# A two-layer decoder trunk on one core: rests shared otherwise, scaling in steps, gathered rows moved from one stage to the next

## The chip, the cores and the metric

The kernel runs on one core of a Trainium2 chip. Five engines work side by side, each with its own queue of instructions: TensorE (PE, with its weight loads as PEld), VectorE (DVE), ScalarE (ACT), GpSimd (POOL) and SyncE (SP). Transfers are issued from the queues of SP, ACT and POOL. The metric is the time of one execution on the device, in microseconds; less is better.

## The reference, cut to what matters

Two layers over 256 positions of width 1024. The even layer's mixer is attention and retention, the odd layer's a short gated convolution; after each mixer comes PEER, a retrieval of 16 out of 16384 experts for each of 8 heads.

```python
def short_conv_mixer(xn, w_in, conv_w, w_out):
    bg, cg, hx = jnp.split(xn @ w_in, 3, axis=-1)
    u = cg * hx
    y = lax.conv_general_dilated(u, conv_w[:, None, :], ...)
    return (bg * y) @ w_out

def peer(xn, w_q, sub_keys, u, v):
    q = (t @ w_q).reshape(n_tok, PEER_HEADS, 2, PEER_DKEY // 2)
    sc = jnp.einsum('thpd,hpnd->thpn', q, sub_keys).astype(jnp.float32)
    s1, i1 = lax.top_k(sc[:, :, 0], PEER_TOPK)
    s2, i2 = lax.top_k(sc[:, :, 1], PEER_TOPK)
    ...
    eidx = jnp.take_along_axis(cidx, pos, axis=-1)
    gate = jax.nn.softmax(top_s, axis=-1).astype(xn.dtype)
    ...
        hid = jax.nn.gelu(jnp.einsum('td,thkd->thk', tc, u[ec]), approximate=False)
        return jnp.einsum('thk,thkd->td', gc * hid, v[ec])
```

So each token needs, for its 128 chosen experts, a product with a row of u, a GELU, a gate, and a weighted sum of rows of v. All values are float32.

## The kernel before, in words

The 256 tokens are treated in two ways. For 160 of them (`TD`) PEER is computed densely: the whole of u and of v, 128 tiles each of 128 experts, goes through TensorE, and the gates of experts that were not chosen are zero. For the other 96 (`TG`) the rows of the chosen experts are gathered from memory by index. 96 gathered steps for u and 96 for v make 192 steps in a layer; each step brings 128 rows of 4 KB (0.5 MB, as much as one tile of u or v).

The order of the work is written out by hand; each engine runs its instructions in the order of the program. The stages of a layer are:

- **Mixer** (even or odd). Weights come as float32 tiles `raw`, at most eight at a time, and each is split into a part `hi` that TensorE takes at a higher rate (ScalarE, L144) and a rest `lo` in bf16 (L146). Whether VectorE or GpSimd subtracts the rest is the second entry of a tile's source: True means GpSimd. For the odd mixer's W_in that is the list on L210. The splits run two tiles ahead of TensorE's use, four in the mixers.
- **Joint.** At the end of a stage four quarters of the sum are added to h, each followed by `norm.done(a, ...)`; the new h is transposed (`turn`) and split with its gain (`parts`) into x2, the operand of the next stage. `amid` runs between two parts of the last quarter, and `tail` finishes inside the first pair of projections of the next stage (`u_pair`).
- **Queries.** Sixteen projections with W_q, scores against the sub-keys, and top-k on VectorE. `rows` (L473) makes the dense tokens' operand XF and the gathered tokens' XG, at the second projection.
- **u stage.** For each tile i of u: eight matmuls (L1223), GELU on ScalarE, and from about the 60th tile on the gate matrices G (L1186), which need one-hot masks from VectorE (L1178). Meanwhile `Gather.step` consumes gathered rows: VectorE multiplies a row (L866 for u, L881 for v), and POOL issues the row that takes its buffer (L856), six buffers in all. How many steps are consumed at each tile is set by `ga.rate`, so that about `UPTO` are done before the last eleven tiles.
- **v stage.** For each tile of v, 40 of 128 are multiplied whole (L1312), at four passes; 88 (`SPL`) are split into vhi (ScalarE, L1234) and vlo (VectorE, L1241), and the hidden rows likewise into hs and hb (ScalarE, L1288 and L1289) and a rest of hs (VectorE, L1293, `row_rest`), and multiplied in two kinds of matmul (L1316 with hs, L1318 with hb). Parts are made three tiles ahead (`AHEAD`). The gathered steps that remain are consumed here at an even rate; then everything is folded into h.

Of the kernel before, what the change touches and what calls it, by code (L numbers as in the profile page):

```python
# [9 lines left out]
F32 = mybir.dt.float32  # L10
# [4 lines left out]
OP = mybir.AluOpType  # L15
# [3 lines left out]
P = 128  # L19
S = 256  # L20
D = 1024
ND = D // P
# [5 lines left out]
NK = 128  # L28
# [6 lines left out]
TG = 96  # L35
TD = S - TG
STEPS = TG
SUB = 32
# [2 lines left out]
MORE = 4  # L41
GT = 4
SCR = 11 * D
UPTO = 132
SPL = [i for i in range(NK) if i % 2 or i % 16 in (4, 8, 12)]
CODE = 64.0
WHOLE = 1.5 * 2.0 ** 23
PRE = {5 * k: k for k in range(11)} | {58: 14, 64: 15, 70: 11, 76: 16, 82: 18, 88: 12, 94: 17, 100: 13, 106: 19}
# [2 lines left out]
CALM = 11  # L51
# [51 lines left out]
class Stream:  # L103
# [28 lines left out]
    def whole(self, i):  # L132
        return self.srcs[i][1] is None
# [49 lines left out]
def trunk_kernel(ctx, tc, x, small, cst, mcst, ew_in, ew_out, ow_in, ow_out, wq, keys, pu, pv, pun, gains, out):  # L183
    nc = tc.nc
    v = nc.vector
    act = nc.scalar
    gp = nc.gpsimd
# [8 lines left out]
    srcs = []  # L196
# [10 lines left out]

    srcs += peer_srcs(0)
    OF = [b * ND + k for k in range(ND) for b in (1, 2, 0)]
    srcs += [(ow_in[f], i not in (1, 2) and i % 4 != 3) for i, f in enumerate(OF)]  # L210
    srcs += [(ow_out[c], c % 2 == 0 and c < 6) for c in range(ND)]
    srcs += peer_srcs(1)

    h = pers.tile([P, 2, D], F32, tag="h", name="h")
# [6 lines left out]
    XF = pers.tile([P, ND, TD], F32, tag="xf", name="xf")  # L221
    XG = pers.tile([P, 2, D], F32, tag="xg", name="xg")
# [5 lines left out]
    def hid_tile(name):  # L228
        return ps_hid.tile([P, 512], F32, tag="hid", name=name)
# [9 lines left out]
    def nm(s):  # L239
        uid[0] += 1  # L240
        return f"{s}{uid[0]}"
# [17 lines left out]
    def u_pair(A2, Ab, tail):  # L259


        ws = [st.next(ahead=False) for _ in range(2)]
        pss = [hid_tile(nm("hid")) for _ in range(2)]
        for k in range(ND):
            for s_ in range(2):
                for (hi, lo), ps in zip(ws, pss):
                    pe.matmul(ps[:, :S], hi[:, k * P:(k + 1) * P], A2[:, k, s_, :], start=k == 0 and s_ == 0,
                              stop=False)
            if k == 0:
                tail()  # L270
                st.ahead(0)
        for (hi, lo), ps in zip(ws, pss):
            for k in range(ND):
                pe.matmul(ps[:, :S], lo[:, k * P:(k + 1) * P], Ab[:, k, :], start=False, stop=k == ND - 1)
        return pss
# [58 lines left out]
    def new_x2():  # L334
        xv["x2"] = pers.tile([P, ND, 2, S], F32R, tag="x2", name=nm("x2"))

    class Sums:


        def __init__(self):  # L340
            self.w = pers.tile([P, 2, 8], F32, tag="nw", name=nm("nw"))
# [29 lines left out]
    class Norm(Sums):  # L371
# [3 lines left out]
        def __init__(self, gi):  # L375
            super().__init__()
            self.gi = gi
            self.ps = {}
            self.turned = False

        def warm(self):

# [29 lines left out]
        def done(self, a, junk):  # L412

            if a == 1:
                self.turn(0)
            if a < 3:
                self.square(a, junk)
            if a == 1:
                self.mean0(0)
                self.root(0)  # L420
            if a == 2:
                self.turn(1)
                self.rstd(0)
                self.mean0(1)
                new_x2()
            if a == 3:
                if not self.turned:
                    self.turn(2)
                self.parts(0)
                self.junk = junk  # L430

        def amid(self):

            self.turn(2)
            self.turned = True

        def tail(self):

            self.turn(3)
            self.parts(1)  # L440
            self.square(3, self.junk)
            self.root(1)
            self.rstd(1)
# [28 lines left out]

        def rows(self):  # L473

            ps = self.spread()
            x2 = xv["x2"]
            v.tensor_tensor(XF, x2[:, :, 0, TG:].bitcast(F32), x2[:, :, 1, TG:].bitcast(F32), OP.add)
            v.tensor_tensor(XF, XF, ps[:, None, TG:].to_broadcast([P, ND, TD]), OP.mult)
            v.scalar_tensor_tensor(XG[:TG, 0, :], h[:TG, 0, :], self.scale(0)[:TG], XG[:TG, 1, :],
                                   op0=OP.mult, op1=OP.mult)  # L480
            act.copy(XG[:TG, 1, :], XG[:TG, 0, :])
            for q in range(2):
                gp.dma_start(XG[TG:, q, :], XG[q * SUB:(q + 1) * SUB, 0, :])

    class Final(Sums):

# [10 lines left out]
        def gained(self, a, eng):  # L497
            th, c = a // 2, slice(a % 2 * 512, (a % 2 + 1) * 512)
            eng.tensor_tensor(self.xs[:, th, c], h[:, th, c], self.g[:, c], OP.mult)

        def done(self, a, junk):
            self.square(a, junk)
# [400 lines left out]
    def peer(l, before, norm):  # L903
        with tc.tile_pool(name=nm("hg"), bufs=1) as hp:
            HG = hp.tile([P, NK, TD], F32, tag="hg", name=nm("hg"))
# [35 lines left out]
            ga = Gather(hp)  # L941
# [56 lines left out]
            def stage1(th, f0, f1):  # L998
                def g():
                    top16([(V[th][:, f * TK:(f + 1) * TK], IU[th][:, f * TK:(f + 1) * TK],  # L1000
                            sc(th, f)) for f in range(f0, f1)])
                return g
# [129 lines left out]
            for f in range(NPAIR):  # L1132
                if f == 0:
                    pair = u_pair(xv["x2"], Xb, before.tail)
                ps = pair[f] if f < 2 else u_tile(xv["x2"], Xb)
                act.copy(qT[f % 2], ps[:, :S])
                if f == 1:
                    before.rows()
                if f:
                    scores(f - 1)  # L1140
                    pump.add((1.35, stage1(0, f - 1, f)))
                    if f <= HH * 2:
                        pump.add((1.35, stage1(1, f - 1, f)))
                    if f == HH * 2:
                        chain(0, 0)
                        pump.add((0.6, lambda: places(0)))
                    if early:
                        fetch(early.pop(0))
                pump.run(3.2)
# [48 lines left out]
            gst = {"g": -1, "credit": 0.0, "rate": 0.0}  # L1198
# [45 lines left out]
            for i in range(NK):  # L1244
                ps = dense_u(i)
                if i == 0:
                    after_first()
                elif early_u:
                    fetch(early_u.pop(0))
                if i == NK - 1:  # L1250
                    gst["rate"] = 1.0
                    while gst["g"] < NG:
                        slot(i)
                T = max(gst["g"], 0) * GT
                if T < TD:
                    act.activation(HG[:, i, T:], ps[:, T:TD], AF.Gelu)  # L1256
                if T > 0:
                    act.activation(ps[:, :T], ps[:, :T], AF.Gelu)
                    v.tensor_tensor(HG[:, i, :T], ps[:, :T], HG[:, i, :T], OP.mult)  # L1259
                slot(i + 1)  # L1260
                if gst["g"] < 0:
                    if i == first_late - 2:
                        pump.flush()
                    if pump.q:
                        pump.run(1.4)
                    else:
                        gst["g"] = 0
                        gst["rate"] = NG / (2.0 * (NK - 8 - i))
                        onehots(0)
                        onehots(1)  # L1270
                ga.rate = 0.85 if gst["g"] < 0 else (UPTO - ga.c) / (NK - CALM - i) if i < NK - CALM else 0.6
                if i < NK - QUIET:
                    ga.step()
                elif i in (NK - QUIET, NK - QUIET + 2):
                    weight_parts(i - NK + QUIET + 1)
# [14 lines left out]

            def row_rest(j):
                hs = hsb[j][0]
                v.tensor_tensor(hs[:, 1, :], HG[:, j, :], hs[:, 0, :].bitcast(F32), OP.subtract)  # L1293

            for j in (1, 3):
                row_parts(j)
                row_rest(j)
            for i in range(NK):
                j = i + AHEAD
                if 4 <= j and j in SPL:  # L1300
                    weight_parts(j, False)
                    row_parts(j)
                if 4 <= j - 1 and j - 1 in SPL:
                    weight_rest(j - 1)
# [4 lines left out]
                m = dict(start=i == 0, skip_group_check=True)  # L1309
                if i not in SPL:  # L1310
                    for b in range(ND):
# [18 lines left out]
            for a in range(4):  # L1330
                th, ch = a // 2, a % 2
                for b in range(4):
                    pe.transpose(fq[a][:, b * P:(b + 1) * P], OT[:, ch * 4 + b, th * P:(th + 1) * P], ident)
                c = slice(ch * 512, (ch + 1) * 512)
                v.tensor_tensor(h[:, th, c], fq[a], h[:, th, c], OP.add)
                norm.done(a, fq[a])
            vpool.close()

    with tc.manual_schedule():
# [12 lines left out]
        a = Norm(1)  # L1352
# [3 lines left out]
        a = Norm(3)  # L1356
# [40 lines left out]
```

## Time and profile before

| | |
|---|---|
| median of 3 runs | 1529.94 us (1529.59 to 1531.46) |
| the profiled execution | 1531.33 us, its span 1529.6 us |
| TensorE busy | 1468.2 us, 96% of the span |
| VectorE, ScalarE, GpSimd busy | 1206.3, 790.9 and 676.0 us |
| moved by DMA | 533.03 MB, 348 GB/s on average |

TensorE's busy time counts pipelined records that overlap, so 96% does not mean that it runs at its peak; the pace of equal records tells more. In lines of the groups the columns are the source line, the engine, the operation, what it writes and reads, the count, the busy time, the mean duration of one in ns, and the idle time before it with what ended it.

### The profile page before, as it was taken

Reading aid. Unit: us, or ns where it says so; the run is one execution under the profiler, and the core shown is the slowest. Engines: PE = TensorE matmul, PEld = TensorE weight load, DVE = VectorE, ACT = ScalarE, POOL = GpSimd, SP = SyncE. Lnnn points to the kernel's source line nnn. Section 1 sums busy time; section 2 is a strip of 40 time slices with the busy share of each in tenths; the row PEclk is TensorE's granted clock in tenths of the full one; section 3 lists DMA queues with packets and bytes.
Section 4 is the critical chain, followed back from the end, with each engine's and each line's share of the span. In section 5 each row is a group of like instructions: output and inputs, shape, how many; then the busy total and the mean of one; then the engine's idle time right before and its main releaser. Section 6 shows DMA issues by size and latency. Waiting matters only on the chain.

```text
span 1529.6 us, 30523 instructions
## 1 busy us (share of the span) xinstructions
PE 1468.2 (96%) x11094; PEld 1375.5 (90%) x11108; DVE 1206.3 (79%) x2561; ACT 790.9 (52%) x2020; POOL 676.0 (44%) x521
## 2 busy tenths in 40 slices
PE   9999999989999999999979999999899999999997
PEld 5667999989999999999969789999899999999996
DVE  5647999868898787777785589996778887787886
ACT  5555512158777354545553463213787754555454
POOL 6744544446655232322046364454556652323310
PEclk9999999999999999999989999999999999999998
DMA  8544899999999999999955568999999999999993
GB/s 320 198 143 178 318 408 408 398 404 408 407 397 409 372 402 375 399 403 393 323 185 194 187 222 332 408 408 400 407 407 405 406 396 383 407 399 402 407 394 127
DMA packets 147576, 533.03 MB, mean 348 GB/s; under 512 B 16993, under 2 KB 17249, under 8 KB 147425
## 3 DMA queue, kind: packets, MB, share of 16 engines
q1 hardware_dynamic: 72144, 258.36, 44.1%
q0 software_dynamic: 56704, 205.07, 34.2%
q10 hardware_dynamic: 18576, 67.64, 11.4%
q8 instruction: 88, 1.44, 0.4%
q14 instruction: 64, 0.52, 0.1%
HBM read 528.34 MB, written 1.05 MB: 346 GB/s over the span
## 4 chain that ended last, share of the span: by engine, by line
PE 35%; DMA 32%; DVE 23%; issue 7%; ACT 2%; POOL 1%; ACTq 0%; DVEq 0%; POOLq 0%
DMA raw<-pv 14%; DMA rows<-pun,ig 7%; PE vo L1316 7%; DMA rows<-pv,ig 6%; PE vo L1312 5%; PE hid L1223 5%; DMA grow<-pun,ig 4%; DVE rows L866 3%; PE vo L1318 3%; PE hid L250 3%; DVE hg L982 2%; DVE grow L866 2%; PE ea L284 2%; DVE hg L988 2%; DVE hg L984 2%
## 5 line engine op out<-in xcount | busy, mean ns | idle before, releaser
L1223 PE MATMUL hid<-xf,raw 128*128 128x160 f32 x3456 | 492.3, 301 | 0.2
L1223 PEld LDWEIGHTS hid<-xf,raw 128*128 128x128 f32 x3456 | 478.7, 192 | 0.8 <-issue 0.5
L1234 ACT CAST vhi<-raw 128x1024 fp32r<-128x1024 f32 x176 | 184.2, 1046 | 231.6 <-DMA raw<-pv 176.3
L1241 DVE TENSOR_TENSOR vlo<-raw,vhi 128x1024 bf16<-128x1024 f32 x176 | 215.4, 1224 | 109.5 <-ACT vhi L1234 86.0
L856 POOL DMA_INDIRECT rows<-pv,ig x128 | 158.8, 1241 | 268.5 <-DVE gacc L881 233.7
L1316 PE MATMUL vo<-hs,vhi 128*128 128x320 f32 x1408 | 251.6, 320 | 6.1 <-DVE hs L1293 5.9
L146 POOL TENSOR_TENSOR lo<-raw,hi 128x1024 bf16<-128x1024 f32 x75 | 178.3, 2394 | 90.1 <-ACT hi L144 88.2
L1316 PEld LDWEIGHTS vo<-hs,vhi 128*128 128x128 f32 x1408 | 208.9, 188 | 9.2 <-DVE hs L1293 9.1
L856 POOL DMA_INDIRECT rows<-pun,ig x128 | 156.1, 1219 | 130.5 <-DVE rows L866 85.1
L1312 PE MATMUL vo<-hg,raw 128*128 128x160 f32 x1280 | 190.5, 302 | 0.9 <-DVE hg L1259 0.9
L866 DVE SCALAR_TENSOR_TENSOR rows<-rows,xg 128x1024 f32<-128x1024 f32 x128 | 155.6, 1220 | 39.1 <-DMA rows<-pun,ig 36.1
L1312 PEld LDWEIGHTS vo<-hg,raw 128*128 128x128 f32 x1280 | 176.3, 190 | 1.2 <-DVE hg L1259 1.2
L1256 ACT ACTIVATE hg<-hid 128x160 f32<-128x160 f32 (+25 forms) x242 | 63.1, 269 | 210.5 <-PE hid L1223 165.1
L881 DVE SCALAR_TENSOR_TENSOR gacc<-rows,ghid,gacc 128x1024 f32<-128x1024 f32 x124 | 158.7, 1279 | 10.2 <-DMA rows<-pv,ig 9.4
L1177 ACT ACTIVATE ko<-ko,idxT 128x128 f32<-128x128 f32 x320 | 130.8, 481 | 0.0
L856 POOL DMA_INDIRECT grow<-pv,ig x64 | 77.0, 1203 | 118.3 <-DVE gacc L881 99.4
L1318 PE MATMUL vo<-hb,vlo 128*128 128x160 bf16 x1408 | 128.3, 234 | 0.0
L1174 ACT ACTIVATE ko<-cst,idxT 128x128 f32<-128x128 f32 x320 | 103.1, 391 | 36.3 <-PE G L1186 31.9
L250 PE MATMUL hid<-x,hi 128*128 128x256 f32 x800 | 108.9, 289 | 6.7 <-issue 6.7
L144 ACT CAST hi<-raw 128x1024 fp32r<-128x1024 f32 x100 | 102.6, 1048 | 19.0 <-issue 10.1
L1186 PE MATMUL G<-ko 128*128 128x128 f32 x640 | 89.3, 284 | 24.0 <-DVE ko L1178 23.7
L1318 PEld LDWEIGHTS <-vlo 128*128 128x128 bf16 x1408 | 93.5, 98 | 18.0
(228 smaller groups left out, 2116.9 us busy)
## 6 DMA issues: line engine op xcount, KB each, us to landing
raw<-pu SPq DMA_DIRECT2D x216, 512.0 KB
raw<-pv SPq DMA_DIRECT2D x128, 512.0 KB
raw<-pv ACTq DMA_DIRECT2D x128, 512.0 KB
raw<-wq SPq DMA_DIRECT2D x32, 512.0 KB
raw<-ew_in SPq DMA_DIRECT2D x28, 512.0 KB
raw<-ow_in SPq DMA_DIRECT2D x24, 512.0 KB
hg<-pu SPq DMA_DIRECT2D x22, 512.0 KB
raw<-ew_out SPq DMA_DIRECT2D x8, 512.0 KB
```

The lines of the kernel that those rows point to most:

```text
L146: eng.tensor_tensor(lo, t, hi.bitcast(F32), OP.subtract)
L250: pe.matmul(ps[:, :S], hi[:, k * P:(k + 1) * P], A2[:, k, s_, :], start=k == 0 and s_ == 0, stop=False)
L856: gp.indirect_dma_start(self.row(s_), None, table, bass.IndirectOffsetOnAxis(IG[:, 0, s_ % STEPS:s_ % STEPS + 1].bitcast(U32), 0))
L866: v.scalar_tensor_tensor(r, r, 1.0, XG[:, q % 2, :], op0=OP.mult, op1=OP.mult, accum_out=w)
L881: v.scalar_tensor_tensor(self.acc[q], r, w, self.acc[q], op0=OP.mult, op1=OP.add)
L1177: act.activation(B[:, j], B[:, j], AF.Relu, bias=idxT[:, 2, t:t + 1], scale=idxT[:, 3, t:t + 1])
L1223: pe.matmul(ps[:, :TD], w[k], XF[:, k, :], start=k == 0, stop=k == ND - 1)
L1234: act.copy(whi[j], raw)
L1241: v.tensor_tensor(wlo[j], raw, whi[j].bitcast(F32), OP.subtract)
L1312: pe.matmul(vo[b][:, :TD], w[:, b * P:(b + 1) * P], HG[:, i, :], stop=False, **m)
L1316: pe.matmul(vo[b][:, :2 * TD], hi[:, b * P:(b + 1) * P], hs, stop=i == NK - 1, **m)
L1318: pe.matmul(vo[b][:, :TD], lo[:, b * P:(b + 1) * P], hb, stop=i == NK - 1, **m)
```

## The change: what it does

- `UPTO` becomes (126, 119), one number a layer, instead of 132 for both; with the few steps after it 130 and 123 steps are done in the u stages instead of 136, and 62 and 69 are left for the v stages instead of 56. Early in u the rate is 0.6 for eight tiles and then 0.88, instead of 0.85.
- `SPL` splits 95 tiles of v instead of 88.
- The rest of the hidden rows (`row_rest`) is subtracted by GpSimd, 190 times in all; VectorE had 176.
- In the odd mixer the rests of the first seven tiles of W_in all go to VectorE, and after that every second one to GpSimd: 9 of 24, where it had 16.
- `rows` gives back four steps, which run at the third to sixth projection, one at each.
- `tail` is called after two of eight steps of the first pair instead of one; `amid` makes the first two of the first four parts of x2, and is now also called at PEER's end, ahead of the last add.

```diff
-UPTO = 132
-SPL = [i for i in range(NK) if i % 2 or i % 16 in (4, 8, 12)]
+UPTO = (126, 119)
+SPL = [i for i in range(NK) if i % 2 or i % 4 == 0 and i > 0]
...
-    srcs += [(ow_in[f], i not in (1, 2) and i % 4 != 3) for i, f in enumerate(OF)]
+    srcs += [(ow_in[f], i > 6 and i % 2 == 1) for i, f in enumerate(OF)]
...
-            if k == 0:
+            if k == 1:
                 tail()
                 st.ahead(0)
...
             if a == 3:
-                if not self.turned:
-                    self.turn(2)
-                self.parts(0)
+                self.parts(0, (2, 3))
                 self.junk = junk
 
         def amid(self):
 
             self.turn(2)
-            self.turned = True
+            self.parts(0, (0, 1))
...
         def rows(self):
 
-            ps = self.spread()
             x2 = xv["x2"]
-            v.tensor_tensor(XF, x2[:, :, 0, TG:].bitcast(F32), x2[:, :, 1, TG:].bitcast(F32), OP.add)
-            v.tensor_tensor(XF, XF, ps[:, None, TG:].to_broadcast([P, ND, TD]), OP.mult)
-            v.scalar_tensor_tensor(XG[:TG, 0, :], h[:TG, 0, :], self.scale(0)[:TG], XG[:TG, 1, :],
-                                   op0=OP.mult, op1=OP.mult)
-            act.copy(XG[:TG, 1, :], XG[:TG, 0, :])
-            for q in range(2):
-                gp.dma_start(XG[TG:, q, :], XG[q * SUB:(q + 1) * SUB, 0, :])
+
+            def whole():
+                v.tensor_tensor(XF, x2[:, :, 0, TG:].bitcast(F32), x2[:, :, 1, TG:].bitcast(F32), OP.add)
+
+            def scaled():
+                ps = self.spread()
+                v.tensor_tensor(XF, XF, ps[:, None, TG:].to_broadcast([P, ND, TD]), OP.mult)
+
+            def fetched():
+                v.scalar_tensor_tensor(XG[:TG, 0, :], h[:TG, 0, :], self.scale(0)[:TG], XG[:TG, 1, :],
+                                       op0=OP.mult, op1=OP.mult)
+
+            def doubled():
+                act.copy(XG[:TG, 1, :], XG[:TG, 0, :])
+                for q in range(2):
+                    gp.dma_start(XG[TG:, q, :], XG[q * SUB:(q + 1) * SUB, 0, :])
+
+            return [fetched, doubled, whole, scaled]
...
                 if f == 1:
-                    before.rows()
+                    rows = before.rows()
+                if 1 < f < 6:
+                    rows[f - 2]()
...
-                ga.rate = 0.85 if gst["g"] < 0 else (UPTO - ga.c) / (NK - CALM - i) if i < NK - CALM else 0.6
+                ga.rate = (0.6 if i < 8 else 0.88) if gst["g"] < 0 else (UPTO[l] - ga.c) / (NK - CALM - i) if i < NK - CALM else 0.6
...
             def row_rest(j):
                 hs = hsb[j][0]
-                v.tensor_tensor(hs[:, 1, :], HG[:, j, :], hs[:, 0, :].bitcast(F32), OP.subtract)
+                gp.tensor_tensor(hs[:, 1, :], HG[:, j, :], hs[:, 0, :].bitcast(F32), OP.subtract)
...
                 c = slice(ch * 512, (ch + 1) * 512)
+                if a == 3:
+                    norm.amid()
                 v.tensor_tensor(h[:, th, c], fq[a], h[:, th, c], OP.add)
                 norm.done(a, fq[a])
```

More of the change, by code (lines that the diff above doesn't have):

```diff
@@ L378, in __init__ @@
             self.ps = {}
-            self.turned = False
         def warm(self):
@@ L499, in gained, with amid @@
             eng.tensor_tensor(self.xs[:, th, c], h[:, th, c], self.g[:, c], OP.mult)
+        def amid(self):
+            pass
         def done(self, a, junk):
```

## The prediction

> **What bounds the kernel now.** I read the page first (busy shares, data rate by slice), then the stretches of the stages, then the waits of TensorE, then the chain.
>
> ```profile
> span 1529.6 us, 30523 instructions
> PE 1468.2 (96%) x11094; PEld 1375.5 (90%) x11108; DVE 1206.3 (79%) x2561; ACT 790.9 (52%) x2020; POOL 676.0 (44%) x521
> GB/s 320 198 143 178 318 408 408 398 404 408 407 397 409 372 402 375 399 403 393 323 185 194 187 222 332 408 408 400 407 407 405 406 396 383 407 399 402 407 394 127
> ...
> 184.00:519.60 335.60, 322.94 (x2380) 320.81 (x2379) 283.70 (x698) 172.51 (x568) 176.89 (x150) 0.98 1.01 398
> 519.60:745.00 225.40, 219.73 (x1829) 209.83 (x1828) 179.67 (x216) 116.49 (x241) 60.52 (x51) 1.00 1.00 387
> 519.60:771.30 251.70, 246.03 (x2050) 234.93 (x2048) 196.25 (x236) 131.49 (x271) 63.41 (x53) 1.00 0.98 377
> 935.70:1269.60 333.90, 320.43 (x2381) 317.84 (x2380) 283.11 (x698) 171.90 (x567) 174.17 (x150) 0.99 1.01 399
> 1269.60:1490.00 220.40, 219.08 (x1829) 209.64 (x1828) 178.34 (x216) 117.72 (x241) 62.79 (x51) 1.00 1.01 399
> 1269.60:1516.30 246.70, 245.38 (x2050) 234.72 (x2048) 194.98 (x237) 130.71 (x269) 63.32 (x52) 1.00 0.95 373
> ```
>
> A stretch row gives its bounds, its length, busy time of PE, PEld, DVE, ACT and POOL, granted clock, DMA share and GB/s. 184 to 519.6 and 935.7 to 1269.6 are the two u stages (128 tiles of u, L1223), 519.6 to 771.3 and 1269.6 to 1516.3 the two v stages (L1312, L1316, L1318). They are 1168 of 1530 us, and in them both TensorE (over 95% busy) and the DMA (about 400 GB/s, where the slices never pass 409) are full. Taking 408 as the ceiling, one tile or gathered row of 0.524 MB costs 1.285 us of it.
>
> ```profile
> 344.97 0.89 PE G L1186 x8
> 345.86 3.26 PE hid L1223 x24
> 538.76 2.22 PE vo L1312 x16
> 540.98 1.17 PE vo L1316 x8
> 542.15 0.57 PE vo L1318 x8
> ...
> 546.27 2.21 PE vo L1312 x16
> ...
> 550.23 1.81 PE vo L1312 x13
> ```
>
> This is the chain where TensorE alone sets the pace (start, length). A u tile is 16 records of 0.136 us, 2.17 us; with 40 groups G of 0.89 us a u stage needs 128 x 2.17 + 36 = 314 us, and takes 335.6 and 333.9. In v, one whole and three split tiles take 546.27 - 538.76 = 7.51 us, one of each 550.23 - 546.27 = 3.96 us. Sixteen tiles of before are 3 x 7.51 + 2 x 3.96 = 30.45, so a v stage needs 243.6 us and takes 251.7 and 246.7.
>
> ```profile
> PE G L1186 <- DVE ko L1178: 23.7, 11, 6.2
> PE hid L250 <- issue: 6.7, 1, 6.7
> PE vo L1316 <- DVE hs L1293: 5.9, 8, 1.4
> PE sc L993 <- DVE xf L478: 3.0, 2, 1.5
> PE hid L267 <- DVE x L407: 2.1, 3, 0.9
> PE fq L1333 <- DVE xg L1328: 2.0, 2, 1.8
> ```
>
> TensorE's waits (total, times, longest) name the places that the change touches: the one-hot masks of G, one hole in the odd mixer, the row rests, the tokens' scaling, the joints between stages.
>
> **Odd mixer: rests shared otherwise.** GpSimd had 16 of the 24 rests `lo` of W_in, VectorE 8; now GpSimd has 9, all from the eighth tile on.
>
> ```profile
> 766.96 2.36 POOL L146 TENSOR_TENSOR lo<-raw,hi 128x1024 bf16<-128x1024 f32 x1 [18.10 <-ACT hi L144]
> 767.91 2.48 DVE L146 TENSOR_TENSOR lo<-raw,hi 128x1024 bf16<-128x1024 f32 x1 [1.00 <-ACT hi L144]
> 770.32 2.47 DVE L889 TENSOR_TENSOR h<-gacc,h 96x1024 f32<-96x1024 f32 x2
> ...
> 792.78 2.41 POOL L146 TENSOR_TENSOR lo<-raw,hi 128x1024 bf16<-128x1024 f32 x1
> 793.13 8.07 DVE L146 TENSOR_TENSOR lo<-raw,hi 128x1024 bf16<-128x1024 f32 x1 [0.52 <-ACT hi L144]
> 795.48 4.63 POOL L146 TENSOR_TENSOR lo<-raw,hi 128x1024 bf16<-128x1024 f32 x2
> 801.64 1.62 PE L250 MATMUL hid<-x,hi 128*128 128x256 f32 x6 [6.72 <-issue]
> L1241 DVE TENSOR_TENSOR vlo<-raw,vhi 128x1024 bf16<-128x1024 f32 x176 | 215.4, 1224 | 109.5 <-ACT vhi L1234 86.0
> ```
>
> The same VectorE subtraction takes 1.22 us in the v stages (L1241) and 8.07 us at 793.13, where GpSimd runs three subtractions back to back until 800.1: VectorE stood still while GpSimd worked. That is the 6.7 us hole. With the first seven rests on VectorE no GpSimd subtraction is there: -6.7. At 767.91 the same collision delays the fold (L889, then xg, which ends the stage) by 2.48 - 1.22 = 1.26: -1.2. VectorE gets seven more rests (7 x 1.22 = 8.6 us), which the tiles' look-ahead covers; the nine left on GpSimd may still block it by up to 2.4 each, so I take +0.4. Sum -7.5; ends -9 and -4.
>
> **Scaling in steps.** The same four operations move from one place to four successive projections. They held the score tile for 1.5 us per layer (waits, L478): -2.5; if the later step finds VectorE backlogged as much, 0, or +1. The copies' DMAs move two projections later on POOL's queue; the rows that need them are issued only after the last projections' top-k.
>
> **Joints.** `amid` now also makes two quarters of x2, ahead of the last add to h; `tail` comes one step later in the pair. The operations are the same. TensorE waits 2.1 us there in three places; what is won at the first matmul is partly lost at the add: -1 (ends -2.5 and +2).
>
> **Rows out of u.** In the changed program's order of instructions the rows consumed by tile 60, where G begins, go from 52 to 51; by tile 116 from 129 to 124 and 117; by the end from 136 to 130 and 123.
>
> ```profile
> DVE rows L866 <- DMA rows<-pun,ig: 20.4, 20, 1.3
> DVE grow L866 <- DMA grow<-pun,ig: 8.6, 8, 1.9
> PE G L1186 <- DVE ko L1178: 12.3, 7, 5.3
> PE G L1186 <- DVE ko L1178: 11.4, 4, 6.2
> ```
>
> The first three are the second u stage, the last the first one. VectorE waits for rows to land, the masks behind it come late, TensorE waits for them. The longest wait is G's first, and one row less before it is worth at most one transfer: -1.5 each. What remains is 11.4 - 6.2 = 5.2 and 12.3 - 5.3 = 7.0. Four rows fewer in that stretch free 4 x 1.285 = 5.1 us of DMA, eleven free 14.1: I take -4 and, bounded by the waits, -7. Sum -5.5 and -8.5; ends 0 and, if the small gaps up to 314 go too, -20 for both.
>
> **v: seven more split tiles, 6 and 13 more rows, row rests on GpSimd.** TensorE: 31 x 7.51 + 2 x 3.96 = 240.7, so -2.9 where it binds. Data: 6 x 1.285 = 7.7 and 13 x 1.285 = 16.7 us more, all before the rows end at tile 114. Up to there the first layer runs at 387 GB/s, so 225.4 x (1 - 387/408) = 11.6 us of DMA lie free and cover 7.7. In the second 220.4 x (1 - 399/408) = 4.9 lie free; 16.7 - 4.9 = 11.8, less two transfers that a u stage no longer full of rows lands earlier: +9. I take 0 and +9, ends -3 and +5, 0 and +14.
>
> The row rest has no row on GpSimd. The nearest:
>
> ```profile
> L146 POOL TENSOR_TENSOR lo<-raw,hi 128x1024 bf16<-128x1024 f32 x75 | 178.3, 2394 | 90.1 <-ACT hi L144 88.2 <-DMA hg<-pu 1.2 <-PE acc L285 0.6
> L499 POOL TENSOR_TENSOR ko<-h,xf 128x512 f32<-128x512 f32 x2 | 2.5, 1276 | 24.0 <-DVE h L1335 24.0
> L1293 DVE TENSOR_TENSOR hs<-hg,hs 128x160 fp32r<-128x160 f32 x176 | 55.9, 319 | 0.0
> L881 DVE SCALAR_TENSOR_TENSOR gacc<-rows,ghid,gacc 128x1024 f32<-128x1024 f32 x124 | 158.7, 1279 | 10.2 <-DMA rows<-pv,ig 9.4
> ```
>
> 2.18 ns per element between the two sizes gives 0.51 us for 160, against 0.32 on VectorE. On POOL's queue it stands ahead of the row's issue and behind the one before, which waits for VectorE's accumulate; on VectorE it stood behind that accumulate too, so the order costs nothing new. 190 x 0.32 = 61 us leave VectorE; if each blocks VectorE for 0.51, 97 us come back. I book nothing beyond the data: VectorE is busy 80% of a v stage.
>
> The Trainium skill ("SBUF — State Buffer", section "SBUF: two separate sides") says that VectorE and GpSimd share a port pair as an exclusive lock, and that a VectorE operation with two SBUF inputs and a GpSimd one that reads SBUF wait for each other in full. The rows at 793.13 agree; by it the rival "one lane" below would hold.
>
> **Sum** against this execution (1531.33 us, 1.39 above the median 1529.94): -7.5 - 2.5 - 1 - 14 + 9 = -16: 1515.3, or 1514 as a median.
>
> **Rivals.**
> - One lane: VectorE's two-input operations and the row rests exclude each other. The lane needs 95 x (1.224 + 0.507) = 164.4 plus 62 or 69 rows x 1.279 = 79.3 or 88.3, and some 8 us stand empty after the rows end: 252 and 261 us, +0.2 and +14.2 instead of 0 and +9. Time 1519. For it: 793.13. Against: at 80% busy much falls into idle time.
> - Data covered: gathered rows run six ahead, the weight ring eight; v costs nothing in layer two, and layer one gets the -2.9. Time 1514 - 9 - 3 = 1502. Against it: 399 GB/s.
> - Rows change nothing in u (weights take the freed DMA time, masks stay late): 1514 + 14 = 1528, no change.
> - Slower: the row rest is already what TensorE waits for in v (L1316 <- hs). On GpSimd it must first wait for the subtraction or accumulate that VectorE is in, half of 1.22 us on average. From 16/190 = 0.08 us exposed per split tile it eats all gains; 0.6 us on every third is 63 x 0.6 = 38: 1552.
>
> **How the numbers follow.** Forecast 45%, one lane 15%, covered 15%, rows change nothing 7%, late row rests 18%. 0.2% is 3.1 us, about what this kernel's runs can tell. Faster: 45 + 15 + 15 + 2 = 77%; same 5%; slower 18%. The range runs from the covered case to the unchanged one, 1502 to 1530; the slower case lies outside. The forecast's own is 1507 to 1521.
>
> **What the changed profile would show.** The 6.7 us wait at L250 gone; u stages of 330 and 325 us with TensorE's waits for masks under 8 each; v stages near 252 and 256 at 405 GB/s; GpSimd's row rests near 0.5 us, and VectorE's L1241 still near 1.22 (near 1.7: one lane). Wrong if TensorE's wait for hs grows past 16 us.

## The result and the profile after

The changed kernel takes 1519.74 us (median of 4 runs, 1516.96 to 1521.56) against 1529.97 us before: a ratio of 0.993, with a 95% interval of 0.9913 to 0.9947. The forecast was 1514, in a range of 1502 to 1530. The profiled execution took 1520.15 us with a span of 1518.4.

The page of the changed kernel, first its span, its engines and its data rate in 40 slices, then its groups:

```profile
span 1518.4 us, 30875 instructions
PE 1461.4 (96%) x11108; PEld 1364.2 (90%) x11108; DVE 1218.0 (80%) x2406; ACT 812.0 (53%) x2062; POOL 891.7 (59%) x704
GB/s 314 196 153 207 288 406 409 397 407 409 407 401 409 390 401 409 395 395 393 337 217 198 150 321 335 409 407 397 385 394 393 392 380 392 408 407 400 403 393 141
...
L1253 DVE TENSOR_TENSOR vlo<-raw,vhi 128x1024 bf16<-128x1024 f32 x190 | 246.7, 1303 | 88.6 <-ACT vhi L1246 87.6
...
L1305 POOL TENSOR_TENSOR hs<-hg,hs 128x160 fp32r<-128x160 f32 x190 | 202.4, 1072 | 51.0 <-ACT hs L1300 47.8
...
L891 DVE SCALAR_TENSOR_TENSOR gacc<-rows,ghid,gacc 128x1024 f32<-128x1024 f32 x124 | 171.5, 1383 | 5.8 <-DMA rows<-pv,ig 5.4
```

VectorE gave away 176 row rests (55.9 us) and is busier than before (1206.3 to 1218.0 us). Seven rests more in the odd mixer and 14 more in v, at 1.22 us each, are 25.6 us of it; besides, its weight rests went from 1224 to 1303 ns and its accumulates from 1279 to 1383. GpSimd's row rest takes 1072 ns on average, twice the 0.51 us worked out from its size.

The four long stages of the changed kernel, in the same columns as in the prediction (bounds, length, busy time of PE, PEld, DVE, ACT and POOL, granted clock, DMA share, GB/s):

```profile
183.35:508.84 325.49, 318.29 (x2381) 317.19 (x2380) 275.97 (x692) 171.68 (x568) 162.19 (x144) 0.99 1.01 399
508.84:764.70 255.86, 245.63 (x2050) 231.72 (x2048) 210.22 (x163) 142.89 (x292) 187.94 (x153) 1.00 1.01 388
919.54:1243.91 324.37, 317.89 (x2380) 317.43 (x2379) 267.12 (x685) 172.76 (x568) 163.46 (x136) 0.99 1.00 391
1243.91:1505.60 261.69, 247.49 (x2050) 233.21 (x2048) 219.31 (x170) 140.16 (x289) 192.74 (x161) 0.99 0.97 376
```

TensorE's waits in the changed kernel (total, times, longest):

```profile
PE vo L1328 <- POOL hs L1305: 23.6, 31, 2.1
PE G L1198 <- DVE ko L1190: 13.4, 5, 6.4
PE hid L250 <- DVE cg L812: 1.3, 1, 1.3
PE sc L1003 <- DVE xf L479: 1.2, 2, 0.6
```

The u stages went from 335.6 and 333.9 to 325.5 and 324.4 us, the v stages from 251.7 and 246.7 to 255.9 and 261.7. Together that is 1167.9 before and 1167.4 after: nothing. The gain lies elsewhere: the 6.7 us hole in the odd mixer is gone, and the score tile's wait for scaling fell from 3.0 to 1.2. In v, TensorE's wait for the row rest went from 5.9 to 23.6 us, past the 16 us that the prediction named as its sign of being wrong. By this page alone one would put the growth of v down to GpSimd. The runs say otherwise.

### The profile page after: what moved, and what is told of

Read it like the earlier page. It is cut to its first block, busy times and chain, and to the rows that moved or that the text cites. A ratio compares the mean times of both kernels' runs of the same rounds, so it can differ in the third digit from the quotient of the medians.

```text
span 1518.4 us, 30875 instructions
## 1 busy us (share of the span) xinstructions
PE 1461.4 (96%) x11108; PEld 1364.2 (90%) x11108; DVE 1218.0 (80%) x2406; ACT 812.0 (53%) x2062; POOL 891.7 (59%) x704
## 4 chain that ended last, share of the span: by engine, by line
PE 50%; DVE 23%; DMA 18%; issue 4%; POOL 3%; ACT 2%; ACTq 0%; SPq 0%; POOLq 0%; DVEq 0%
PE hid L1235 17%; DMA raw<-pv 13%; PE vo L1328 7%; PE G L1198 4%; PE vo L1324 4%; DMA rows<-pun,ig 4%; DVE rows L876 3%; PE vo L1330 3%; PE hid L250 3%; DVE hg L992 2%; DVE hg L998 2%; DVE hg L994 2%; DVE grow L876 2%; PE ea L286 2%; PE ea L285 2%
## 5 line engine op out<-in xcount | busy, mean ns | idle before, releaser
L1246 ACT CAST vhi<-raw 128x1024 fp32r<-128x1024 f32 x190 | 198.9, 1047 | 227.5 <-DMA raw<-pv 155.6
L1253 DVE TENSOR_TENSOR vlo<-raw,vhi 128x1024 bf16<-128x1024 f32 x190 | 246.7, 1303 | 88.6 <-ACT vhi L1246 87.6
L1328 PE MATMUL vo<-hs,vhi 128*128 128x320 f32 x1520 | 272.8, 321 | 23.9 <-POOL hs L1305 23.6
L1328 PEld LDWEIGHTS vo<-hs,vhi 128*128 128x128 f32 x1520 | 226.0, 189 | 31.8 <-POOL hs L1305 31.7
L866 POOL DMA_INDIRECT rows<-pv,ig x128 | 177.2, 1384 | 100.6 <-DVE gacc L891 44.5
L1305 POOL TENSOR_TENSOR hs<-hg,hs 128x160 fp32r<-128x160 f32 x190 | 202.4, 1072 | 51.0 <-ACT hs L1300 47.8
L146 POOL TENSOR_TENSOR lo<-raw,hi 128x1024 bf16<-128x1024 f32 x68 | 163.2, 2415 | 76.8 <-ACT hi L144 73.8
L891 DVE SCALAR_TENSOR_TENSOR gacc<-rows,ghid,gacc 128x1024 f32<-128x1024 f32 x124 | 171.5, 1383 | 5.8 <-DMA rows<-pv,ig 5.4
L1324 PE MATMUL vo<-hg,raw 128*128 128x160 f32 x1056 | 157.2, 302 | 0.5 <-DVE hg L1271 0.5
L1324 PEld LDWEIGHTS vo<-hg,raw 128*128 128x128 f32 x1056 | 145.5, 190 | 0.8 <-DVE hg L1271 0.8
L866 POOL DMA_INDIRECT grow<-pun,ig x64 | 75.7, 1183 | 87.9 <-DVE grow L876 52.0
```

The costliest lines, as they stand in the source:

```text
L146: eng.tensor_tensor(lo, t, hi.bitcast(F32), OP.subtract)
L866: gp.indirect_dma_start(self.row(s_), None, table, bass.IndirectOffsetOnAxis(IG[:, 0, s_ % STEPS:s_ % STEPS + 1].bitcast(U32), 0))
L891: v.scalar_tensor_tensor(self.acc[q], r, w, self.acc[q], op0=OP.mult, op1=OP.add)
L1246: act.copy(whi[j], raw)
L1253: v.tensor_tensor(wlo[j], raw, whi[j].bitcast(F32), OP.subtract)
L1305: gp.tensor_tensor(hs[:, 1, :], HG[:, j, :], hs[:, 0, :].bitcast(F32), OP.subtract)
```

## The experiments

Each run also has runs of the kernel before on its chip beside it; their medians were 1528.95, 1529.96 and 1530.00 us for the three groups in which they ran. Single executions of one kernel lie up to some 12 us apart, so a profiled stage is read to a few us only. Theories A to E are those of the texts of what was expected.

**The row rests back on VectorE.**

```diff
 # the changed kernel
-                gp.tensor_tensor(hs[:, 1, :], HG[:, j, :], hs[:, 0, :].bitcast(F32), OP.subtract)
+                v.tensor_tensor(hs[:, 1, :], HG[:, j, :], hs[:, 0, :].bitcast(F32), OP.subtract)
```

> The changed kernel with its 190 row rests put back on VectorE, nothing else undone. Theory A (the late row rest): the 4 and 15 us that the v stages grew by are TensorE's waits for row rests on GpSimd (23.6 us in the changed kernel, 5.9 before). Then those waits fall to 4 to 8 us, the v stages come back to about 243 to 248 us each, VectorE's weight rests to 1.22 us, and the time to 1519.7 - 17 = about 1503 (1498 to 1508). Theory B (the data): the v stages are longer because 6 and 13 more gathered rows pass through them; then they stay near 256 and 262 us with TensorE waiting for weights or accumulates instead, and the time stays at 1518 to 1522. Theory C (VectorE full): 61 us more on VectorE make it the bound of v, which ends near 252 to 258; the time is 1512 to 1520.

1519.15 us (0.9936, 0.9917 to 0.9955): no difference to the changed kernel. Its stages and its wait, with the row rest on VectorE again:

```profile
508.22:763.38 255.16, 246.09 (x2050) 231.87 (x2048) 213.95 (x258) 142.67 (x292) 81.08 (x58) 1.00 1.01 390
...
1241.74:1503.44 261.70, 247.20 (x2050) 232.04 (x2048) 220.38 (x265) 139.40 (x289) 92.34 (x66) 1.00 0.97 375
```

```profile
PE vo L1328 <- DVE hs L1305: 22.1, 32, 2.0
```

The same 22 us, the same stages, though the row rest is back at 319 ns:

```profile
L1253 DVE TENSOR_TENSOR vlo<-raw,vhi 128x1024 bf16<-128x1024 f32 x190 | 232.3, 1223 | 83.2 <-ACT vhi L1246 70.4 <-PE vo L1328 6.7 <-PE vo L1330 5.3
...
L1305 DVE TENSOR_TENSOR hs<-hg,hs 128x160 fp32r<-128x160 f32 x190 | 60.4, 319 | 0.1
```

So theory A fell. The row rest is only the last link. The chain of this run, in a stretch of its second v stage (start, length, what), shows what stands before it:

```profile
1371.80 8.04 DMA raw<-pv
...
1379.94 1.06 ACT vhi L1246
1381.00 0.02 issue
1381.02 0.26 DVE vlo L1253
...
1382.16 0.33 DVE hs L1305
1382.49 0.04 issue
1382.53 1.44 PE vo L1328 x8
```

The weight tile needs 8 us to land; then ScalarE rounds it, VectorE makes its rest (1.23 us, of which this chain counts 0.26), then the row rest queued behind it, and TensorE starts 0.04 us after that. TensorE's wait "for hs" is here a wait for data with three instructions in between. Over the whole of this stage 53% of the chain is the landing of v's tiles; VectorE's rests, accumulates and row rests are 10% of it.

**Only the row rests on GpSimd.**

```diff
 # the kernel before
-                v.tensor_tensor(hs[:, 1, :], HG[:, j, :], hs[:, 0, :].bitcast(F32), OP.subtract)
+                gp.tensor_tensor(hs[:, 1, :], HG[:, j, :], hs[:, 0, :].bitcast(F32), OP.subtract)
```

> The kernel before with only its 176 row rests moved to GpSimd. Theory A: each waits about 0.5 us or more behind VectorE's two-input operations, TensorE's waits for them grow from 5.9 to 15 to 25 us, GpSimd's row rest shows about 1 us instead of the 0.5 worked out from its size, and the time is 1530 + 9 to 19 = 1539 to 1549. Theory B: the row rests cost nothing by themselves, since the rows are those of before; 1527 to 1532.

1534.21 us (1.0033, 1.0019 to 1.0046): 5 us slower, less than A expected and more than B. TensorE's waits for hs stay at 6.6 us and the row rest takes 1149 ns. Its profiled execution took 1532.1 us, only 0.8 above that of the kernel before, with v stages of 249.4 and 249.8 us (0.7 more in sum), so it can't show where the 5 us go. In the changed kernel the same edit costs nothing; why it costs here stays open.

**Only the odd mixer's share.**

```diff
 # the kernel before
-    srcs += [(ow_in[f], i not in (1, 2) and i % 4 != 3) for i, f in enumerate(OF)]
+    srcs += [(ow_in[f], i > 6 and i % 2 == 1) for i, f in enumerate(OF)]
```

> The kernel before with only the odd mixer's weight rests shared as in the changed kernel. The prediction's step: the 6.7 us hole at the hidden matmuls goes and the fold comes 1.2 us earlier, -7.5 (ends -9 and -4), so 1522.5 (1521 to 1526). Rival: with seven more rests and without the other joints VectorE is late elsewhere and half of the gain is lost, 1526 to 1529.

1523.02 us (0.9961, 0.9948 to 0.9975): -5.9. In its profile the stretch from the first transposes of the odd mixer to the next ones is 93.1 us, against 100.3 before, with TensorE busy for nearly all of it:

```profile
771.50:864.58 93.08, 90.79 (x688) 78.34 (x689) 63.68 (x110) 41.85 (x61) 39.12 (x27) 1.00 0.62 199
```

Before, in the same columns:

```profile
775.38:875.68 100.30, 92.89 (x687) 80.95 (x689) 62.74 (x104) 41.98 (x61) 52.17 (x33) 0.95 0.53 186
```

The 5.9 us are over half of the whole change's gain.

**Only the rows.**

```diff
 # the kernel before
-UPTO = 132
+UPTO = (126, 119)
-                ga.rate = 0.85 if gst["g"] < 0 else (UPTO - ga.c) / ...
+                ga.rate = (0.6 if i < 8 else 0.88) if gst["g"] < 0 else (UPTO[l] - ga.c) / ...
```

> The kernel before with only the rows moved from u to v (130 and 123 consumed in u instead of 136, with the other pace at the start), row rests still on VectorE and the old split tiles. The changed kernel's u stages are 10.1 and 9.5 us shorter than before. Theory A (in v the rows cost nothing): u 325 to 327 us each, v 248 to 254 us each, time 1530 - 19 = 1509 to 1515. Theory B (the rows' data lengthen v): u the same, v +4 and +15 us, time 1527 to 1531. If the shorter u comes from another edit than the rows: u stays at 333 to 336 and the time at 1528 to 1532.

1531.31 us (1.0016, 1.0002 to 1.003): the rows' two terms in the prediction, -14 and +9, make -5, and nothing of it came. Its four stages:

```profile
184.79:510.07 325.28, 317.98 (x2381) 316.84 (x2380) 276.23 (x692) 171.75 (x567) 162.04 (x144) 0.99 1.01 399
510.07:764.79 254.72, 248.06 (x2050) 235.20 (x2048) 203.25 (x243) 132.56 (x271) 78.20 (x59) 1.00 1.00 389
928.79:1252.14 323.35, 317.22 (x2380) 316.76 (x2379) 266.99 (x685) 172.99 (x568) 164.27 (x136) 0.99 1.01 393
1252.14:1513.57 261.43, 249.82 (x2050) 235.46 (x2048) 211.76 (x251) 129.89 (x268) 84.82 (x66) 1.00 0.97 376
```

All four are those of the changed kernel within 1.2 us, with the rows alone. u and v together take 580.0 and 584.8 us, against 587.3 and 580.6 before. What u wins, v gives back.

**The changed kernel with the old rows** (and row rests on VectorE).

```diff
 # the changed kernel, row rests on VectorE
-UPTO = (126, 119)
+UPTO = (132, 132)
-                ga.rate = (0.6 if i < 8 else 0.88) if gst["g"] < 0 else ...
+                ga.rate = 0.85 if gst["g"] < 0 else ...
```

> The changed kernel with the row rests back on VectorE and the old pace of the rows (136 consumed in u), so that odd share, steps, joints and split tiles remain. Theory D (one sum of data): in u and v together the same 448 transfers of a layer pass one DMA ceiling, so that moving rows between the stages changes nothing; u 333 to 336, v 246 to 252, u plus v as in the run with rests on VectorE (580.4 and 585.1) within 3 us, time 1517 to 1522. Theory E (fewer rows in u is a gain of its own, as predicted -14 against +9): 5 us worse or more, 1524 to 1530.

1517.81 us (0.9916, 0.9896 to 0.9936), level with the 1519.15 of the run with the new rows. Its u stages are 333.8 and 333.0 us, its v stages:

```profile
516.45:763.36 246.91, 243.69 (x2050) 231.51 (x2048) 206.96 (x252) 141.71 (x292) 60.87 (x52) 1.00 1.01 389
...
1251.29:1499.17 247.88, 244.07 (x2050) 231.64 (x2048) 204.89 (x251) 140.45 (x290) 68.04 (x52) 1.00 0.97 374
```

Beside it, the new rows cost v 8.3 and 13.8 us (255.16 and 261.70 against these two) and save u 8.6 and 9.6. Theory E, 1524 or more, is out. Theory D, one sum of data for u and v, fits: u and v together take 580.7 and 580.9 us here, 580.3 and 585.1 with the new rows (the second layer differs by 4.2, more than the 3 that D allowed). A layer's 128 tiles of u, 128 of v and 192 rows are 448 transfers, 448 x 1.285 = 576 us of the ceiling, and its two stages took 574 to 587 us in the profile of every run that makes these 448.

**Only the scaling in steps.**

```diff
 # the kernel before
-                    before.rows()
+                    rows = before.rows()
+                if 1 < f < 6:
+                    rows[f - 2]()
```

> The kernel before with only the fetched tokens' scaling in four steps. The prediction's step: -2.5 (ends -3 and +1), so 1526.5 against 1529, with the query stages going from 60.0 to 58.4 us each as in the changed kernel. Rival: the later step finds VectorE as backlogged, no change. If the query stages stay at 60.0, their 1.6 us each in the changed kernel come from the joints.

1527.69 us (0.9979, 0.9966 to 0.9992): -2.3. The query stages are 58.6 us each, and the score tile's wait for the scaling is 1.2 us, not 3.0.

**Only the split tiles.**

```diff
 # the kernel before
-SPL = [i for i in range(NK) if i % 2 or i % 16 in (4, 8, 12)]
+SPL = [i for i in range(NK) if i % 2 or i % 4 == 0 and i > 0]
```

> The kernel before with only the seven more split tiles. Theory D (v waits for data): TensorE's floor falls by 2.9 us a layer but the data do not, so -0 to -2 in all, 1528 to 1530. If TensorE binds v: -5.8, 1524. If joints and split tiles together are the 4 us by which the run with the old rows stands below the sum of odd share and steps, this run shows which: about 1526 where it is the split tiles.

1529.90 us (0.9992, 0.9975 to 1.001): nothing, as D has it. TensorE's floor of 240.7 us, which this edit lowers, isn't what v ends by.

This run also speaks to a rival of D. A moved row brings not only 1.285 us of data to v but also an accumulate of 1.28 us on VectorE, so the growth of v alone doesn't tell the two apart. Here VectorE works 9 us longer in each v stage than before (205.1 and 204.4 us against 196.3 and 195.0), with the data as they were, and the two stages take 499.4 us against 498.4. So v hardly grows with VectorE's work; at most the 2.9 us a stage by which TensorE's floor fell could hide some of it.

**v's rows spread towards its end.**

```diff
 # the changed kernel, row rests on VectorE
-            ga.rate = (ga.TOTAL - ga.c) / (NK - 14.0)
+            ga.rate = (ga.TOTAL - ga.c) / (NK - 7.0)
```

> The changed kernel with row rests on VectorE and v's rows spread to seven tiles before the end instead of fourteen. Theory D: the data are what v waits for up to its tile 114, and in the last 50 us only 281 to 283 GB/s of about 408 are moved; some three rows a layer go from the crowded stretch into the free one, v shortens by 2 to 5 us a layer, time 1509 to 1516. If v waits for VectorE or for the row rests themselves and not for data: 1517 to 1522, and above 1522 if the late accumulates delay the fold.

1513.37 us (0.9894, 0.9869 to 0.9918), the lowest median of the runs that do the whole work, 5.8 below the 1519.15 without the spreading. Five of its six executions lie below all of that run's and one above, and the intervals just touch, so the gain is likely rather than certain. v takes 249.3 and 258.1 us instead of 255.2 and 261.7. The last 51.6 us of the two v stages, first with rows until fourteen tiles before the end, in the order second and first stage, then the same of this run:

```profile
1451.84:1503.44 51.60, 49.55 (x416) 46.84 (x414) 38.98 (x50) 27.68 (x59) 5.81 (x5) 1.00 0.76 283
711.78:763.38 51.60, 51.45 (x432) 48.61 (x430) 41.95 (x51) 31.81 (x64) 4.29 (x4) 1.00 0.96 349
```

```profile
1444.43:1496.03 51.60, 50.81 (x426) 47.81 (x424) 44.59 (x54) 27.18 (x59) 11.73 (x9) 1.00 0.80 314
706.52:758.12 51.60, 51.47 (x432) 48.64 (x431) 45.03 (x54) 31.92 (x64) 8.38 (x7) 1.00 1.00 383
```

The DMA, which had room at the stage's end, is busier there (0.76 to 0.80, 0.96 to 1.00), with TensorE as full as before or fuller, and the stretch ahead of it is relieved of these rows, of their data and of their accumulates alike.

**The same with the old rows,** and then with GpSimd's row rests (each diff is the one shown above).

> The run with the old rows (row rests on VectorE, 136 rows consumed in u), with v's rows spread to seven tiles before the end. Theory D: u 333, v 243 to 246 a layer instead of 247 and 248, so 1510 to 1515 and level with the run that spreads the changed kernel's rows. If v's rows are already free there (TensorE's floor 240.7): no change, 1516 to 1519.

> The kernel with the old rows spread to seven tiles before the end, its row rests on GpSimd. Alone on the kernel before, GpSimd's row rests cost 5 us (ratio 1.0033); in the changed kernel they cost nothing (1519.7 against 1519.2 with VectorE). Where v waits less for data, theory A says that they show again: 3 to 8 us above the same kernel with rests on VectorE, 1515 to 1521. Theory D says that they lie beside the waits for data: within 2 us of it.

1516.82 us (0.9917, 0.9898 to 0.9936) and 1515.50 us (0.9912, 0.9896 to 0.9928). With the old rows the spreading gives 1.0 us against 1517.81, which is no gain that these runs can tell: D's 1510 to 1515 is missed, and the other case of that text, no change, is what came. v stood at 246.9 and 247.9 already and comes to 246.4 and 245.4, with TensorE busy for 98.5% and 99.0% of it, so little was left to win. GpSimd's row rests cost nothing here either, in v stages of 244.1 and 246.3 us: theory A's 3 to 8 us aren't there.

**Transfers added and taken away.** Eight of v's gathers a layer twice, in the kernel before; eight left out, in the changed kernel with row rests on VectorE.

```diff
 # added
+                for _ in range(2 if s_ in range(140, 180, 5) else 1):
                     gp.indirect_dma_start(self.row(s_), None, table, ...)
 # left out
+                if s_ in range(140, 180, 5):
+                    continue
                 gp.indirect_dma_start(self.row(s_), None, table, ...)
```

> The kernel before with eight of v's row gathers of each layer issued twice (the same rows into the same buffer), 16 transfers of 0.524 MB more in all, nothing computed otherwise. Theory D: each costs its 1.285 us of the ceiling, +20 (1544 to 1551). If v had room for rows, as the prediction's first layer says (11.6 us free there, 4.9 in the second): 0 and +5, so 1532 to 1536.

> The changed kernel with row rests on VectorE and with eight of v's row gathers of each layer left out (their products take the row that stands in the buffer from earlier, so those eight rows' part of the output is not the reference's; VectorE and TensorE do the same work). Theory D: each transfer left out gives its 1.285 us back, v 255.2 - 10 = 245 and 261.7 - 10 = 251.5, time 1519 - 20 = 1497 to 1502. Theory C (VectorE or the row rests bind v, not the data): v unchanged, 1516 to 1520.

Added: 1562.48 us (1.021, 1.0186 to 1.0235), +32.5, more than either theory. It isn't a clean price: the second gather into a buffer waits on GpSimd's queue until the first has landed, so later rows are issued late. GpSimd's waits of that run (4.5 us in the kernel before):

```profile
POOL rows L857 <- DMA rows<-pv,ig: 142.3, 12, 19.0
```

Left out: 1504.86 us (0.9838, 0.9817 to 0.9859), -14.3 for 16 transfers, or 0.9 us each instead of 1.285. Its v stages:

```profile
508.67:759.34 250.67, 244.68 (x2050) 231.67 (x2048) 213.48 (x258) 141.66 (x292) 71.72 (x50) 1.00 0.99 381
1239.05:1496.78 257.73, 247.30 (x2050) 232.05 (x2048) 220.16 (x265) 139.07 (x289) 85.60 (x58) 1.00 0.95 365
```

This profiled execution was the slowest of five (1511.59); its v stages are 4.5 and 4.0 us shorter than with all transfers, 0.5 us a transfer. All else was in place, VectorE's accumulates too (213.5 and 220.2 us busy, as with all transfers), so two fifths to seven tenths of a transfer's share of the ceiling lie on v's path. C, by which nothing would change, is out; D in full, 1497 to 1502, is missed as well. u and v together take 575.8 and 582.5 us for 440 transfers, 565 us of the ceiling: with fewer bytes the DMA's rate fell (390 to 381 GB/s in the first v stage) at a share that stayed near 1.0. Why the rest wasn't recovered stays open.

## Why the prediction was right or wrong

The sign and the range held; the sum of -16 came out as -10. By its own steps:

- **Odd mixer, -7.5 (ends -9 and -4): right.** -5.9 by itself, with the hole at L250 gone. VectorE's rests there now take 1.2 us in the median and 2.6 at most, not 8.07.
- **Scaling in steps, -2.5: right.** -2.3 by itself.
- **Joints, -1 (ends -2.5 and +2): not run alone.** With odd share, steps, joints and split tiles the run with the old rows stands 12.2 below the kernel before; the first two make 8.2 of it and the split tiles 0.1. The other 4 are the joints or the spread of the medians.
- **Rows out of u, -5.5 and -8.5: mechanism right in part, too small.** The u stages of the run with only the rows are 10.3 and 10.6 us shorter than before. In the changed kernel TensorE's waits for masks fell from 11.4 to 7.1 and from 12.3 to 6.4 us, which is about half of that. The later waits went as forecast; G's first wait, booked at -1.5 each, stayed (6.2 and 5.3 before, 5.9 and 6.4 after). The other half lies outside these waits.
- **v, 0 and +9: the step that failed.** It said that "11.6 us of DMA lie free and cover 7.7" in the first layer, and 4.9 in the second, because the stage ran at 387 and 399 GB/s under a ceiling of 408. In the run that moves the rows alone against the kernel before, v grew by 3.0 and 14.7 us; against the run with the old rows, with the same other edits, by 8.3 and 13.8. The full price, 7.7 and 16.7, is near that. What v lacked was room in the DMA: VectorE's accumulates, which move with the rows, aren't likely to be the cause, as the run with only the split tiles shows, though a share of theirs isn't excluded. The row quoted for 387 GB/s had a warning in the column before it: a DMA share of 1.00. Here a lower rate at a full share was no free time. The -14 booked for u was then no gain at all, since v gave it back.
- **Split tiles: booked at nothing beyond the data, and nothing came** (-0.1).
- **Row rests on GpSimd: booked at nothing, nothing came in the changed kernel.** The reason was partly wrong, and why the same edit costs 5 us on the kernel before stays open. 0.51 us is only the least (516 ns; the median is 1164), since GpSimd and VectorE stop each other. Of 61 us taken from VectorE some 36 came back: 190 x (1303 - 1223) = 15 on weight rests, 124 x (1383 - 1277) = 13 and 62 x (1399 - 1279) = 7 on accumulates, where the lower figures are those of the run with the rests on VectorE. The prediction's bound for that was 97.

The rival "one lane" gave 1519 and v stages of 252 and 261, close to what was measured, for a reason that isn't the cause: with the row rests taken off that lane the time stays. Its sign was VectorE's weight rest (L1241, in the changed kernel L1253) near 1.7 us, and 1.30 was measured. "Late row rest" had its sign, waits for hs past 16 us, without its mechanism: with VectorE's rests they are 22.1. "Rows change nothing" (1528) was wrong about u, where it expected no gain, and right about the sum of u and v; it was held at 7%.

That the total came within 6 us is partly luck. The rows' two terms, -5 together, came to +2.4 alone (1531.31 against 1528.95), and the joints, or whatever else the 4 us are, gave some 3 us more than booked.

## What to carry to other kernels

Where two stages after one another both run at a DMA share near 1.0, suspect that they are one stage: moving transfers from the one to the other here changed where the wait showed, not when it ended. Look for stretches with a share under 1 and try moving transfers there; it gave 5.8 us with the new rows and 1.0, which can't be told from nothing, where TensorE filled the stage. Don't read a rate under the highest slice as free time when the share is full; but the share doesn't say either what a transfer less will give, since with eight rows out it stayed at 0.99 in the first v stage. And an instruction that an engine waits for can be the last of a chain: to blame it, make it cheap (here 1.07 to 0.32 us) and see whether the wait goes.

## What the runs showed of the hardware

A VectorE subtraction or accumulate and a GpSimd subtraction hold each other up, in short instructions too: a 128x160 subtraction on GpSimd took 516 ns at least, 1164 in the median and 1519 at most, while VectorE's operations with two inputs grew by 6 to 9% beside it. The Trainium skill ("SBUF — State Buffer", section "SBUF: two separate sides") calls the shared ports an exclusive lock held for the whole instruction; these times agree.

The DMA showed a share of 0.99 to 1.01 at anything from 381 to 399 GB/s in the stretches with gathered rows shown here, and its slices reached 409. What lowers the rate there wasn't tested.
